# Sums of weight blocks in a Strassen-style gated layer: from VectorE additions to accumulating transfers in place

## The chip, the cores and the metric

The kernel runs on one core of one Trainium2 chip. The metric is the device time in microseconds (us) of one execution; lower is better. The profile is one execution of the same program with the hardware profiler on.

## The reference

A trunk of two layers over 512 tokens of 1024 channels, all in float32. Each layer has a gated feed-forward half step, four groups of attention heads side by side, and a second feed-forward half step, each followed by a normalisation over the channels:

```python
def _swiglu(h, w_gu, w_down):
    gate, up = jnp.split(h @ w_gu, 2, axis=-1)      # w_gu: 1024 x 5632
    return (jax.nn.silu(gate) * up) @ w_down         # w_down: 2816 x 1024

for l in range(DEPTH):                               # DEPTH = 2
    x = _layer_norm(alpha * x + 0.5 * _swiglu(x, ffn_w_gu[l, 0], ffn_w_down[l, 0]), ...)
    mix = _token_mixers(x, w_in[l], ..., w_out[l], l)
    x = _layer_norm(alpha * x + mix, ...)
    x = _layer_norm(alpha * x + 0.5 * _swiglu(x, ffn_w_gu[l, 1], ffn_w_down[l, 1]), ...)
```

The product `h @ w_gu` of the four feed-forward steps is the place of the change.

## The kernel before, in words

**Seven products in place of eight.** A feed-forward step goes through its 2816 hidden columns in 11 *pairs* of 256 columns (44 pairs in all). For one pair the weight is a 2 x 2 arrangement of blocks: rows 0 to 511 and 512 to 1023 of the input channels (first digit 1 and 2) against gate and up columns (second digit 1 and 2). Each block, called b11, b21, b12 and b22, is 128 partitions x 1024 elements in a tile, 512 KB, loaded by a transfer from the SP queue (`Pair.load`, `load`, L93). The token side is split in halves too, and the products are formed by a scheme of Strassen's kind: products 1 to 7 multiply prepared token combinations (`al1` to `al7`, made once per step) with weight combinations w1 to w7. w1 is b11, w2 is b21, w3 is b22, and the other four are sums: w5 = b11 + b12, w6 = b11 + b12 + b22, w7 = b12 + b22, w4 = b21 + w6.

**Two parts of a weight.** TensorE takes each weight combination as a high part (`wh`, a cast on ScalarE, L351) and a low part (`wl`, the difference, on VectorE, L352); `parts4` makes both. They live in rings of four buffers each (`WB`), so a combination can be split as soon as TensorE is through with the product four places earlier. A product is 24 matmuls of 256 columns: for each of two column halves eight with the high part and four with the low part.

**Buffers and queues.** The raw blocks and the sum `t2` share seven slots in turn (`raw_tile`): three of the pool `raw` and four of the tag `pt`. A block's slot is free for the next load when it was split or added for the last time. Each engine carries out its own instructions in program order, the SP and POOL queues too; which order that is, a scheduler decides when the program is built. The pairs follow one another; `prep12` makes w1 and w2, `prep_rest` the other five, `run12` runs products 1 and 2 and `run_rest` the other five.

**Banks.** Product 1 goes to a bank `a` (in the profile `ga`), which ScalarE copies to `s1`; products 6, 7 and 4 are added on top of it, and ScalarE copies it to `u2` between 6 and 7. Product 2 has the bank `gb`. Products 5 and 3 share the bank `gc`, which ScalarE copies to `p5` between the two. A product that adds onto a bank has to wait for the copy taken before it.

The first two pairs of a step are run in an opening of their own: products 1 and 2 of both come first, while the later token combinations are still being made, and the others after that. After the 11 pairs the down product runs (`acc`), then the normalisation, then the next stage. In the attention stages VectorE, ScalarE and POOL share the work; POOL has nothing to do in the 11 pairs.

Of the kernel before, what the change touches and what calls it, by code (L numbers as in the profile page):

```python
# [14 lines left out]
ALU = mybir.AluOpType  # L15
# [7 lines left out]
FF = 2816  # L23
# [49 lines left out]
def tile_encoder(ctx: ExitStack, tc: tile.TileContext, d: dict, out: bass.AP):  # L73
    nc = tc.nc
    ve, se, ge, te = nc.vector, nc.scalar, nc.gpsimd, nc.tensor

    def pool(name, bufs=1, **kw):
        return ctx.enter_context(tc.tile_pool(name=name, bufs=bufs, **kw))

    cst, st, raw, whi, wlo, blk, sm = (pool("cst"), pool("state"), pool("raw"), pool("whi"), pool("wlo"),  # L80
                                       pool("blk"), pool("small"))
    ps = pool("ps", 2, space=PSUM)
    RAW, WB = 3, 4
    BUFS = {"v": 8, "st": 8, "kr": 1, "hl": 10, "nat": 4, "tb": 3, "o": 2, "od": 1, "o2": 2, "p": 6, "oT": 8}
    NPT = 4
    LAG = 3

# [7 lines left out]
    def block(tag, name, dt=F32, width=512):  # L95
        return blk.tile([P, width], dt, tag=tag, name=name, bufs=BUFS[tag])

# [68 lines left out]
    def alk(n, hl, k):  # L166
        for h, l, k0, nk in al[n]:
            if k0 <= k < k0 + nk:
                return (h if hl == "h" else l)[:, k - k0]
# [75 lines left out]
    def cols_of(w):  # L245
        return w.rearrange("(k p) f -> p k f", p=P)

    def mm(o, a, b, start, stop, **kw):
        te.matmul(o, a, b, start=start, stop=stop, **kw)  # L249
        n = 1  # L250
        for w in b.shape[1:]:
            n *= w
        pe[0] += n / 2400.0
# [62 lines left out]

    TAIL = 4
    NB = NC // 2
    HSLOTS = ["oT"] * 8 + ["nat"] * 4 + ["tb"] * 3 + ["hl"] * 6 + ["v"]
    TMP = ["o", "o", "od", "o2", "o2", "kr"]  # L320

    def ffn(l, f, last, to_next):
        wgu = cols_of(d["ffn_w_gu"][l, f])
        wd = d["ffn_w_down"][l, f]
        ring = {"raw": 0, "tmp": 0}
        slots = list(HSLOTS)
        H = []

        def raw_tile(name):

            ring["raw"] += 1
            if ring["raw"] % 7 in (1, 3, 5):
                return raw.tile([P, DM], F32, tag="r", name=name, bufs=RAW)
            return blk.tile([P, DM], F32, tag="pt", name=name, bufs=NPT)

        def tmp(name):
            ring["tmp"] += 1
            return block(TMP[ring["tmp"] % len(TMP)], name)

        def parts4(r, early=None):  # L340

            if early is None:
                h = whi.tile([P, DM], F32R, tag="h", name="wh", bufs=WB)
                lo = wlo.tile([P, DM], F32R, tag="l", name="wl", bufs=WB)
                pieces = [(h, lo, 0, 4)]
            else:
                pieces = [(block(early, "we", F32R), block(early, "we", F32R), k0, 2) for k0 in (0, 2)]
            out_ = []
            for h, lo, k0, nk in pieces:
                q = slice(k0 * 256, (k0 + nk) * 256)  # L350
                se.copy(h, r[:, q])  # L351
                ve.tensor_tensor(lo, r[:, q], h.bitcast(F32), op=ALU.subtract)  # L352
                out_.append(tuple(w.rearrange("p (k c) -> p k c", c=256) for w in (h, lo)) + (k0, nk))
            return out_

        def product(n, o, w, first):

            for c in range(2):
                seq = []
                for h, lo, k0, nk in w:  # L360
                    for k in range(nk):
                        seq += [(h, k, k0 + k, "h"), (h, k, k0 + k, "l")]
                for h, lo, k0, nk in w:
                    for k in range(nk):
                        seq.append((lo, k, k0 + k, "h"))
                for m, (a, k, kk, hl) in enumerate(seq):
                    mm(o[:, c], a[:, k, c * P:(c + 1) * P], alk(n, hl, kk), first and c == 0 and m == 0,
                       c == 1 and m == len(seq) - 1, skip_group_check=True)

        class Pair:  # L370
# [4 lines left out]
                self.j, self.w, self.r = j, {}, {}  # L375

            def load(self, gate=True, up=True):
                j = self.j
                for n, k, u in ((11, 0, 0), (21, 1, 0), (12, 0, 1), (22, 1, 1)):
                    if not (up if u else gate):  # L380
                        continue
                    self.r[n] = raw_tile(f"b{n}")
                    load(self.r[n].rearrange("p (k c) -> p k c", k=4),
                         wgu[:, 4 * k:4 * k + 4, u * FF + j * 256:u * FF + (j + 1) * 256])
                return self

            def prep12(self, early=(None, None)):
                self.w[1] = parts4(self.r[11], early[0])
                self.w[2] = parts4(self.r[21], early[1])
                return self  # L390

            def prep_rest(self):
                r = self.r
                add = lambda o, a, b: ve.tensor_tensor(o, a, b, op=ALU.add)  # L394
                add(r[11], r[11], r[12])
                t2 = raw_tile("t2")
                add(t2, r[11], r[22])
                self.w[6] = parts4(t2)
                self.w[5] = parts4(r[11])
                add(r[12], r[12], r[22])  # L400
                self.w[7] = parts4(r[12])
                self.w[3] = parts4(r[22])
                add(r[21], r[21], t2)
                self.w[4] = parts4(r[21])
                return self

# [13 lines left out]
            def run_rest(self):  # L420
                v3 = lambda t: t.rearrange("p (c t) -> p c t", c=2)
                a = self.a
                product(6, a, self.w[6], False)
                u2 = v3(tmp("u2"))
                se.copy(u2, a)
                c = self.bank("pj", "gc")
                product(5, c, self.w[5], True)
                p5 = v3(tmp("p5"))
                se.copy(p5, c)
                product(7, a, self.w[7], False)  # L430

                ve.tensor_tensor(p5, a, p5, op=ALU.add)
                product(3, c, self.w[3], False)
                se.activation(self.s1, self.s1, AF.Silu, scale=-1.0)

                ve.tensor_tensor(u2, c, u2, op=ALU.add)
                product(4, a, self.w[4], False)
                h0 = v3(block(slots.pop(0), "h0"))
                ve.tensor_tensor(h0, self.s1, u2, op=ALU.mult)
                s2 = v3(tmp("s2"))  # L440
                se.activation(s2, a, AF.Silu, scale=-1.0)
                h1 = v3(block(slots.pop(0), "h1"))
                ve.tensor_tensor(h1, s2, p5, op=ALU.mult)
                H.append((h0, h1))
# [19 lines left out]
        for j in range(2, NB):  # L464
            p = Pair(j).load().prep12().prep_rest()
# [35 lines left out]
        for t in range(NT):  # L501
            for n in range(2):
                for i in range(TAIL):
                    down(t, NC - TAIL + i, ws[i], (n,))
            layer_norm(t, acc[t], 0.5, gb, last and t == NT - 2)
            if last:
                for n in range(2 if t == NT - 1 else 1):
                    sl = slice(n * FD, (n + 1) * FD) if t == NT - 1 else slice(0, DM)
                    load(out[0, t * P:(t + 1) * P, sl], x[t][:, sl])
            else:  # L510
                to_next[1](t)
# [968 lines left out]
    for l in range(DEPTH):  # L1480
        ffn(l, 0, False, (new_xT, to_xT))
        mixer(l)
        ffn(l, 1, l == DEPTH - 1, (new_al, to_al) if l < DEPTH - 1 else None)
# [22 lines left out]
```

## Time and profile before

| | |
|---|---|
| median of 3 runs | 1987.61 us (1985.27 to 1988.29) |
| profiled execution | 1989.4 us, span 1987.6 us from the first to the last instruction |
| mean granted TensorE clock | 0.983 |
| busy: PE / VectorE / ScalarE / POOL | 1906.2 / 1450.0 / 960.0 / 269.5 us |
| additions of L394 | 88 + 44 + 44 on VectorE, 107.4 + 53.6 + 53.6 us |
| transfers, all from the SP queue | 202.49 MB, 33.7% of the 16 DMA engines' span |

The profile names a tile by its name without the number, so b11, b21, b12 and b22 all read `b`, t2 reads `t`, p5 `p`, u2 `u` and s1 `s`. PE is TensorE, PEld its weight loads, DVE VectorE, ACT ScalarE; SPq is the transfer queue of SyncE.

### The profile page before, as it was taken

To read this page: it belongs to the slowest core of one execution; us is meant where nothing else is said; L and a number is where in the kernel's file an instruction comes from. 1 tells how busy PE (TensorE), PEld (TensorE's weight loads), DVE (VectorE), ACT (ScalarE), POOL (GpSimd) and SP (SyncE) were. 2 spreads that over 40 slices of the span, in tenths; PEclk is the share of its full clock that TensorE was granted. 3 is DMA by queue.
4 is the path that set the end of the run, shared out by engine and by line. 5 is a ranking of instruction groups with operands and counts; after the bars stand their busy time and mean duration, and the time that the engine had idled before them with its cause. 6 is when DMAs were issued, how large, how long until landed. Compare 5 with 4: busy or idle time off the path is not lost.

```text
span 1987.6 us, 31884 instructions
## 1 busy us (share of the span) xinstructions
PE 1906.2 (96%) x12396; PEld 1735.7 (87%) x12396; DVE 1450.0 (73%) x2229; ACT 960.0 (48%) x1593; POOL 269.5 (14%) x411
## 2 busy tenths in 40 slices
PE   7999999999999899999999999999999979999998
PEld 6999988788887899988889999887887869999886
DVE  7887742858999978763598787337689998878535
ACT  5544532248774554443155545322587745444421
POOL 0000000335741000000000000004366300000001
PEclk9999999999999899999999999999999989999999
DMA  5323233343442333332223323331533424232321
GB/s 196 120 88 115 97 101 105 86 112 89 112 112 86 96 110 103 107 127 96 85 77 106 121 92 99 110 120 47 141 93 92 118 74 128 92 112 84 106 97 62
DMA packets 156487, 204.53 MB, mean 103 GB/s; under 512 B 14064, under 2 KB 122608, under 8 KB 156336
## 3 DMA queue, kind: packets, MB, share of 16 engines
q1 hardware_dynamic: 156336, 202.49, 33.7%
q8 instruction: 98, 1.61, 0.3%
q14 instruction: 53, 0.43, 0.1%
HBM read 177.42 MB, written 2.10 MB: 90 GB/s over the span
## 4 chain that ended last, share of the span: by engine, by line
PE 85%; DVE 8%; POOL 2%; ACT 2%; issue 2%; DMA 1%; SPq 0%; DVEq 0%; POOLq 0%; ACTq 0%
PE ga L249 25%; PE acc L249 23%; PE gc L249 13%; PE gb L249 6%; PE nat L249 5%; PE op L249 3%; PE sc L249 3%; PE pjt L249 2%; PE pv L249 2%; PE ptb L109 2%; DVE p L591 1%; PE xtp L109 1%; DVE al L178 1%; POOL wl L222 0%; DVE x L314 0%
## 5 line engine op out<-in xcount | busy, mean ns | idle before, releaser
L249 PE MATMUL ga<-al,wh 128*128 128x256 f32 x2752 | 392.5, 285 | 12.4 <-ACT wh L351 11.7
L351 ACT CAST wh<-b 128x1024 fp32r<-128x1024 f32 x256 | 267.7, 1049 | 280.2 <-issue 164.7
L352 DVE TENSOR_TENSOR wl<-b,wh 128x1024 fp32r<-128x1024 f32 x256 | 311.2, 1219 | 120.9 <-ACT wh L351 120.9
L249 PEld LDWEIGHTS ga<-al,wh 128*128 128x128 f32 x2752 | 360.2, 194 | 13.0 <-ACT wh L351 12.1
L222 DVE TENSOR_TENSOR wl<-wr,wh 128x1024 fp32r<-128x1024 f32 (+1 forms) x92 | 112.2, 1220 | 232.1 <-ACT wh L221 232.1
L249 PE MATMUL acc<-wh,hh 128*128 128x512 f32 x704 | 272.9, 390 | 6.7 <-ACT hh L480 6.7
L249 PE MATMUL acc<-wh,hl 128*128 128x512 f32 x704 | 276.6, 393 | 1.1 <-DVE hl L481 1.1
L249 PE MATMUL acc<-wl,hh 128*128 128x512 f32 x704 | 276.5, 393 | 0.2 <-DVE wl L222 0.2
L221 ACT CAST wh<-wr 128x1024 fp32r<-128x1024 f32 (+2 forms) x98 | 101.5, 1040 | 269.1 <-PE acc L249 226.0
L249 PE MATMUL ga<-al,wl 128*128 128x256 f32 x1376 | 224.3, 286 | 0.0
L303 POOL TENSOR_SCALAR rs<-mv 128x1 f32<-128x1 f32 x24 | 9.9, 412 | 1498.8 <-DVE mv L301 1498.7
L249 PE MATMUL gc<-al,wh 128*128 128x256 f32 x1408 | 201.1, 285 | 4.6 <-ACT al L177 4.3
L249 PEld LDWEIGHTS ga<-al,wl 128*128 128x128 f32 x1376 | 192.2, 194 | 0.6 <-DVE wl L352 0.3
L249 PEld LDWEIGHTS gc<-al,wh 128*128 128x128 f32 x1408 | 184.3, 194 | 5.2 <-ACT al L177 4.5
L249 PEld LDWEIGHTS acc<-wh,hh 128*128 128x128 f32 x704 | 132.1, 188 | 34.5 <-ACT hh L480 7.5
L249 PEld LDWEIGHTS acc<-wh,hl 128*128 128x128 f32 x704 | 133.3, 189 | 30.3 <-DVE hl L481 2.8
L249 PEld LDWEIGHTS acc<-wl,hh 128*128 128x128 f32 x704 | 133.1, 189 | 28.4 <-DVE wl L222 0.6
L249 PE MATMUL gc<-al,wl 128*128 128x256 f32 x704 | 113.6, 284 | 0.0
L394 DVE TENSOR_TENSOR b<-b,b 128x1024 f32<-128x1024 f32 x88 | 107.4, 1220 | 5.5 <-DMA b<-in_ffn_w_gu_dram 4.2
L249 PEld LDWEIGHTS gc<-al,wl 128*128 128x128 f32 x704 | 97.6, 193 | 0.0
L351 ACT CAST wh<-t 128x1024 fp32r<-128x1024 f32 x44 | 46.2, 1049 | 105.6 <-DVE t L394 105.6
L249 PE MATMUL gb<-al,wh 128*128 128x256 f32 x640 | 90.8, 285 | 0.0
(280 smaller groups left out, 3414.6 us busy)
## 6 DMA issues: line engine op xcount, KB each, us to landing
b<-in_ffn_w_gu_dram SPq DMA_DIRECT2D x176, 512.0 KB, 3.6
wr<-in_ffn_w_down_dram SPq DMA_DIRECT2D x88, 512.0 KB, 3.2
wr<-in_w_in_dram SPq DMA_DIRECT2D x30, 512.0 KB, 3.7
k<-ph SPq DMA_DIRECT2D x64, 128.0 KB, 2.4
wr<-in_w_out_dram SPq DMA_DIRECT2D x16, 512.0 KB, 3.6
qs<-ph SPq DMA_DIRECT2D x32, 128.0 KB, 2.4
ln_g<-in_ln_g_dram SPq DMA_DIRECT2D x12, 256.0 KB, 4.1
ln_b<-in_ln_b_dram SPq DMA_DIRECT2D x12, 256.0 KB, 4.7
```

The costliest lines, as they stand in the source:

```text
L109: te.transpose(o, a, ident)
L178: ve.tensor_tensor(l[:, :, cs], v, h[:, :, cs].bitcast(F32), op=ALU.subtract)
L221: se.copy(h[:, w], r[:, w])
L222: (lo or ve).tensor_tensor(l[:, q], r[:, q], h[:, q].bitcast(F32), op=ALU.subtract)
L249: te.matmul(o, a, b, start=start, stop=stop, **kw)
L303: ge.tensor_scalar(rs[:, 0:1], mv[:, 1:2], 1.0, EPS * INV_A * INV_A, op0=ALU.mult, op1=ALU.add)
L351: se.copy(h, r[:, q])
L352: ve.tensor_tensor(lo, r[:, q], h.bitcast(F32), op=ALU.subtract)
L394: add = lambda o, a, b: ve.tensor_tensor(o, a, b, op=ALU.add)
L591: ve.tensor_tensor_reduce(p, sb, nd, -h.slope, h.sink[0] if h.sink else 3.0e38, ALU.add, ALU.min, m)
```

## The change

The four sums are no longer formed by VectorE. Each is an accumulating transfer that POOL issues: it adds its source onto what is in the destination tile. Three of the four read a block of the weights from device memory again, the fourth reads a tile on the chip. The tile `t2` is gone: b11 becomes w5 in place and then w6 in place. `prep_rest` is written in another order, and `run_rest` has product 5 ahead of product 6. One buffer of the tag `hl` is given up, and one more of the tag `v` takes its place in `HSLOTS`; `dynamic_dma_scratch_size`, the room for the descriptors of POOL's transfers, goes from 256 to 2048.

```diff
-    BUFS = {"v": 8, "st": 8, "kr": 1, "hl": 10, ...}
+    BUFS = {"v": 8, "st": 8, "kr": 1, "hl": 9, ...}
...
-    HSLOTS = ["oT"] * 8 + ["nat"] * 4 + ["tb"] * 3 + ["hl"] * 6 + ["v"]
+    HSLOTS = ["oT"] * 8 + ["nat"] * 4 + ["tb"] * 3 + ["hl"] * 5 + ["v"] * 2
...
+            def src(self, u, k):
+                return wgu[:, 4 * k:4 * k + 4, u * FF + self.j * 256:u * FF + (self.j + 1) * 256]
...
+            def add(self, n, src):
+                ge.dma_start(self.r[n].rearrange("p (k c) -> p k c", k=4), src, accum_op=ALU.add)
+
             def prep_rest(self):
-                r = self.r
-                add = lambda o, a, b: ve.tensor_tensor(o, a, b, op=ALU.add)
-                add(r[11], r[11], r[12])
-                t2 = raw_tile("t2")
-                add(t2, r[11], r[22])
-                self.w[6] = parts4(t2)
+                r, b12, b22 = self.r, self.src(1, 0), self.src(1, 1)
+                self.add(12, b22)
+                self.add(11, b12)
                 self.w[5] = parts4(r[11])
-                add(r[12], r[12], r[22])
+                self.add(11, b22)
+                self.w[6] = parts4(r[11])
+                self.add(21, r[11].rearrange("p (k c) -> p k c", k=4))
                 self.w[7] = parts4(r[12])
                 self.w[3] = parts4(r[22])
-                add(r[21], r[21], t2)
                 self.w[4] = parts4(r[21])
...
             def run_rest(self):
-                product(6, a, self.w[6], False)
-                u2 = v3(tmp("u2"))
-                se.copy(u2, a)
                 c = self.bank("pj", "gc")
                 product(5, c, self.w[5], True)
                 p5 = v3(tmp("p5"))
                 se.copy(p5, c)
+                product(6, a, self.w[6], False)
+                u2 = v3(tmp("u2"))
+                se.copy(u2, a)
                 product(7, a, self.w[7], False)
```

ScalarE before, from the split of w7 of one pair (blocks b11_1145, b21_1147, b12_1149, b22_1151) to that of w1 of the next (b11_1373). Behind a tile's name is its number; in brackets are the counters that the instruction waits for (DMAHW a transfer of the SP queue, DMASW one of POOL's):

```order
L351 CAST wh_1173<-b12_1149 128x1024 [waits DMAHW0_49,PE_49,Activation_49]
L414 COPY s1_1211<-ga_1186 128x512 [waits PE_49]
L351 CAST wh_1177<-b22_1151 128x1024 [waits DMAHW1_49,PE_49,Activation_49]
L434 ACTIVATE s1_1211<-s1_1211 128x512 [waits DVE_49]
L351 CAST wh_1182<-b21_1147 128x1024 [waits PE_49,Activation_49]
L425 COPY u2_1263<-ga_1186 128x512 [waits PE_49]
L351 CAST wh_1381<-b11_1373 128x1024 [waits DMAHW2_49,PE_49,Activation_49]
L429 COPY p5_1290<-gc_1265 128x512 [waits PE_49]
```

ScalarE after, the same stretch of the same pair (now b11_1141, b21_1143, b12_1145, b22_1147; the next pair's b11_1368 and b21_1370), and on to the split of that pair's w5:

```order
L351 CAST wh_1169<-b12_1145 128x1024 [waits DMASW6_49,PE_49,Activation_49]
L417 COPY s1_1206<-ga_1181 128x512 [waits PE_49]
L351 CAST wh_1173<-b22_1147 128x1024 [waits DMAHW2_49,PE_49,Activation_49]
L437 ACTIVATE s1_1206<-s1_1206 128x512 [waits DVE_49]
L351 CAST wh_1177<-b21_1143 128x1024 [waits DMASW4_49,PE_49,Activation_49]
L429 COPY p5_1259<-gc_1234 128x512 [waits PE_49]
L351 CAST wh_1376<-b11_1368 128x1024 [waits DMAHW3_49,PE_49,Activation_49]
L432 COPY u2_1285<-ga_1181 128x512 [waits PE_49]
L351 CAST wh_1380<-b21_1370 128x1024 [waits DMAHW1_49,PE_49,Activation_49]
L351 CAST wh_1386<-b11_1368 128x1024 [waits DMASW5_49,DVE_49,PE_49]
```

The cast of w4 (wh_1177) now waits for a transfer of POOL's, and both copies of the pair's banks and the cast of the next pair's w1 stand behind it; p5 and u2 have changed places.

POOL after, from the first sum on b11 of that pair on (before, POOL had no row between the start of the program and the first normalisation):

```order
L395 DMA b11_1141<-in_ffn_w_gu_dram 128x4x256 [waits DMAHW2_49,DMAHW6_49,DMASW1_49,DVE_49]
L395 DMA b12_1372<-in_ffn_w_gu_dram 128x4x256 [waits DMAHW4_49,DMASW0_49]
L395 DMA b11_1141<-in_ffn_w_gu_dram 128x4x256 [waits DMASW1_49,DVE_49]
L395 DMA b21_1143<-b11_1141 128x1024 [waits DMAHW7_49,DMASW3_49]
L395 DMA b11_1368<-in_ffn_w_gu_dram 128x4x256 [waits DMAHW5_49,DMAHW3_49,DVE_49]
L395 DMA b12_1599<-in_ffn_w_gu_dram 128x4x256 [waits DMAHW0_49,DMASW6_49,DMASW4_49]
L395 DMA b11_1368<-in_ffn_w_gu_dram 128x4x256 [waits DMASW5_49,DVE_49]
L395 DMA b21_1370<-b11_1368 128x1024 [waits DMAHW1_49,DMASW7_49]
```

The first sum on a b11 waits for VectorE (the split of w1), the second for the first one's landing and the split of w5, and the sum on b21 for the second one's landing; the sum on the next pair's b12 stands between the first two.

TensorE after, at the products of the same pair: the end of product 6 (bank ga_1181), product 3 (gc_1234) and the first matmul of product 7 (ga_1181). The first row of product 3 needs the copy p5, the first of product 7 the copy u2:

```order
L249 MATMUL ga_1181<-al6_92,wl_1165 128x256 x4
L249 MATMUL gc_1234<-al3_102,wh_1173 128x256 [waits Activation_49]
L249 MATMUL gc_1234<-al3_103,wh_1173 128x256
L249 MATMUL gc_1234<-al3_102,wh_1173 128x256
L249 MATMUL gc_1234<-al3_103,wh_1173 128x256
L249 MATMUL gc_1234<-al3_104,wh_1173 128x256
L249 MATMUL gc_1234<-al3_105,wh_1173 128x256
L249 MATMUL gc_1234<-al3_104,wh_1173 128x256
L249 MATMUL gc_1234<-al3_105,wh_1173 128x256
L249 MATMUL gc_1234<-al3_102,wl_1174 128x256 [waits DVE_49]
L249 MATMUL gc_1234<-al3_102,wl_1174 128x256
L249 MATMUL ga_1181<-al7_93,wh_1169 128x256 [waits Activation_49]
```

Before, the products of a pair stood whole in the order 1, 2, 6, 5, 7, 3, 4; now it is 1, 2, 5, 6, ten matmuls of 3, 7, the other fourteen of 3, and 4.

VectorE before, at the end of the opening of the second step (pair 0 is b11_7005, b21_7007, b12_7009, b22_7011):

```order
L418 TENSOR_TENSOR s1_7119<-gb_7121,s1_7119 128x512 [waits PE_49]
L394 TENSOR_TENSOR b11_7005<-b11_7005,b12_7009 128x1024 [waits DMAHW4_49]
L668 TENSOR_SCALAR nsink_13858<-sink_13857 128x4
L685 TENSOR_SCALAR gd_13869<-gd_13869 128x1
L394 TENSOR_TENSOR t2_7156<-b11_7005,b22_7011 128x1024 [waits DMAHW3_49,DVE_49]
L394 TENSOR_TENSOR b12_7009<-b12_7009,b22_7011 128x1024
L394 TENSOR_TENSOR b21_7007<-b21_7007,t2_7156 128x1024 [waits DVE_49]
L352 TENSOR_TENSOR wl_7159<-t2_7156,wh_7158 128x1024 [waits Activation_49]
```

VectorE after, at the same place (pair 0 is b11_6994, b21_6996, b12_6998, b22_7000):

```order
L421 TENSOR_TENSOR s1_7108<-gb_7110,s1_7108 128x512 [waits PE_49]
L352 TENSOR_TENSOR wl_7147<-b11_6994,wh_7146 128x1024 [waits DMASW5_49]
L671 TENSOR_SCALAR nsink_13825<-sink_13824 128x4
L688 TENSOR_SCALAR gd_13836<-gd_13836 128x1
L352 TENSOR_TENSOR wl_7152<-b11_6994,wh_7151 128x1024 [waits DMASW0_49,Activation_49]
L352 TENSOR_TENSOR wl_7157<-b12_6998,wh_7156 128x1024 [waits DMASW4_49,Activation_49]
```

The four additions are gone, and the low part of w5 stands first where they began; the next one, w6, waits for a transfer that can only start after that.

More of the change, by code (lines that the diff above doesn't have):

```diff
@@ L83, in tile_encoder @@
     RAW, WB = 3, 4
-    BUFS = {"v": 8, "st": 8, "kr": 1, "hl": 10, "nat": 4, "tb": 3, "o": 2, "od": 1, "o2": 2, "p": 6, "oT": 8}
+    BUFS = {"v": 8, "st": 8, "kr": 1, "hl": 9, "nat": 4, "tb": 3, "o": 2, "od": 1, "o2": 2, "p": 6, "oT": 8}
     NPT = 4
@@ L377, in load @@
             def load(self, gate=True, up=True):
-                j = self.j
                 for n, k, u in ((11, 0, 0), (21, 1, 0), (12, 0, 1), (22, 1, 1)):
@@ L382, in load @@
                     self.r[n] = raw_tile(f"b{n}")
-                    load(self.r[n].rearrange("p (k c) -> p k c", k=4),
-                         wgu[:, 4 * k:4 * k + 4, u * FF + j * 256:u * FF + (j + 1) * 256])
-                return self
+                    load(self.r[n].rearrange("p (k c) -> p k c", k=4), self.src(u, k))
+                return self
+            def src(self, u, k):
+                return wgu[:, 4 * k:4 * k + 4, u * FF + self.j * 256:u * FF + (self.j + 1) * 256]
             def prep12(self, early=(None, None)):
@@ L1492 @@
     from concourse.bass_utils import run_bass_kernel_spmd as _run
-    nc = _bacc.Bacc("TRN2", target_bir_lowering=False, num_devices=1, dynamic_dma_scratch_size=256)
+    nc = _bacc.Bacc("TRN2", target_bir_lowering=False, num_devices=1, dynamic_dma_scratch_size=2048)
     arrays, args = {}, {}
```

## Prediction, made before the changed kernel was run

> **What bounds the kernel now.** I read the page's head, then a table by stages, then the chain of work that ended last. First the span, the busy time of each engine, and two stretches of 180 us, one inside the eleven pairs of the first feed-forward step and one inside those of the second:
>
> ```profile
> span 1987.6 us, 31884 instructions
> ...
> PE 1906.2 (96%) x12396; PEld 1735.7 (87%) x12396; DVE 1450.0 (73%) x2229; ACT 960.0 (48%) x1593; POOL 269.5 (14%) x411
> ...
> 60.00:240.00 180.00, 180.00 (x1503) 180.00 (x1502) 142.57 (x146) 91.38 (x113) 0.00 (x0) 1.00 0.32 97
> ...
> 680.00:860.00 180.00, 180.00 (x1503) 180.00 (x1502) 144.97 (x149) 91.22 (x112) 0.00 (x0) 1.00 0.35 108
> ```
>
> The columns of the last two lines are busy us of PE, its weight loads, DVE, ACT and POOL, then granted clock, DMA share and GB/s. In the pairs PE has no gap at all and VectorE is busy 143 of 180 us. So VectorE is not what sets the pace there, and what is taken off it brings nothing by itself. The chain shows the pace, from product 2 of one pair to product 2 of the next:
>
> ```profile
> 107.41 2.88 PE gb L249 x24
> 110.29 2.88 PE ga L249 x24
> 113.17 2.88 PE gc L249 x24
> ...
> 127.57 2.88 PE gb L249 x24
> ```
>
> A product takes 2.88 us and a pair 127.57 - 107.41 = 20.16 us. The open question is whether the sums still come in time at that pace. Outside the steady pairs PE's waits for the work of this change are few; the list of waits (total, times, longest) has
>
> ```profile
> PE xtp L109 <- DVE x L314: 21.4, 8, 6.5
> PE ga L249 <- ACT wh L351: 11.7, 2, 6.0
> ```
>
> The second line is two openings of a step, where the split of w6 comes late behind VectorE's additions.
>
> **What is removed.** Groups by line, with count, busy us and mean ns:
>
> ```profile
> L352 DVE TENSOR_TENSOR wl<-b,wh 128x1024 fp32r<-128x1024 f32 x256 | 311.2, 1219 | 120.9 <-ACT wh L351 120.9
> ...
> L351 ACT CAST wh<-b 128x1024 fp32r<-128x1024 f32 x256 | 267.7, 1049 | 280.2 <-issue 164.7 <-PE ga L249 92.6 <-ACT hh L480 16.4
> ...
> L394 DVE TENSOR_TENSOR b<-b,b 128x1024 f32<-128x1024 f32 x88 | 107.4, 1220 | 5.5 <-DMA b<-in_ffn_w_gu_dram 4.2
> ...
> L394 DVE TENSOR_TENSOR t<-b,b 128x1024 f32<-128x1024 f32 x44 | 53.6, 1219 | 0.1
> L394 DVE TENSOR_TENSOR b<-b,t 128x1024 f32<-128x1024 f32 x44 | 53.6, 1219 | 0.0
> ```
>
> The three L394 groups go: 107.4 + 53.6 + 53.6 = 214.6 us of VectorE, all under a PE without gaps except in the openings. Worth 0 in the steady pairs.
>
> **What is added: three transfers in a row per pair.** By the order of instructions, the second sum on b11 needs the first landed and w5 split, the sum on b21 needs the second landed, and ScalarE has the cast of w4, which needs the sum on b21, ahead of the copy p5, the next pair's cast of w1 and the copy u2. The next pair's first sum on b11 needs w1 split. That closes a loop from pair to pair: cast w4 1.05, copy p5 0.58, cast w1 1.05, difference w1 1.22, transfer, cast w5 1.05, difference w5 1.22, transfer, transfer. The engine part is 6.17 us; 1.05 and 1.22 are from the groups above, 0.58 from
>
> ```profile
> L429 ACT COPY p<-gc x44: 582/582/587, 41.2 to 1847.6; 128x512 f32<-128x512 f32 x44
> ```
>
> With S the sum of the three transfers from issue to landing, the loop takes S + 6.17. It is hidden while that is at most 20.16, so up to S = 14.0, 4.7 us for each. The fourth sum, on b12, is outside the loop: its load is ordered before it is needed and w7 is the fifth product.
>
> No accumulating transfer and none from POOL is in the trace. The nearest rows (KB each, median us from issue to landing), and POOL's own operations:
>
> ```profile
> b<-in_ffn_w_gu_dram SPq DMA_DIRECT2D x176, 512.0 KB, 3.6
> wr<-in_ffn_w_down_dram SPq DMA_DIRECT2D x88, 512.0 KB, 3.2
> ...
> nd_d<-in_nd_d_dram SPq DMA_DIRECT2D x1, 448.0 KB, 9.4
> ...
> 628.13 0.56 POOL L304 TENSOR_TENSOR rs<-rs,mhalf 128x1 f32<-128x1 f32 x1
> ```
>
> From below: a sum costs what the plain load costs, 3.6 from the weights, and 3.2 for the sum on b21, whose rows are 4 KB like those of the second line: S = 10.4. From above: the slowest load of about this size, 9.4 each: S = 28.2. I take a value nearer to the lower end, since the plain loads have the same size, rows and destination. On top of them comes a second pass over 512 KB, because the old content must be read to be added to: the line of 680 to 860 us gives 108 GB/s at a share of 0.35, so 309 GB/s at full share, and 512 KB take 1.7 us. For POOL's issue I add one small operation of its own, 0.56. That is 5.86, 5.86 and 5.46, together 17.2. Of the transfers outside the loop (four loads and the sum on b12) some fall on it: the slot of the next b11 is free when w4 is split, just as the first sum starts, so I add one load's 1.7. S = 18.9, the loop 25.1 us, 4.9 more than a pair takes now.
>
> The Trainium skill ("Collectives: The Full Stack", the section on the bandwidth ceiling) says that an add in the DMA engines costs no cycles but two source reads, which halves the rate; that agrees with taking a second pass, and no run here shows it yet. Its page "DMA: Bandwidth & Descriptors", in the section on the anatomy of a POOL-issued transfer, fits such a transfer as 2.0 us plus bytes at 436 GB/s; an estimate from both is 4.4 us each, 13.2 in all, and the loop would stay just hidden, which is the first rival below. The rows give the dearer answer, and I stay with them.
>
> **How often.** Pairs 1 to 10 of a step are tied by nine loops, 36 in the four steps: 36 x 4.9 = 176 us. In pair 1, w5 can be split only after product 6 of pair 0 (its buffer); from there w5 2.27, two transfers 11.3, w4 1.05 and p5 0.58 make 15.2, against five products, 14.4: 0.8, four times, 3 us.
>
> **The openings.** The end of the second step's opening, VectorE and then TensorE:
>
> ```profile
> 657.16 0.69 DVE L418 TENSOR_TENSOR s<-gb,s 128x512 f32<-128x512 f32 x1
> 657.76 1.22 DVE L394 TENSOR_TENSOR b<-b,b 128x1024 f32<-128x1024 f32 x1
> ...
> 659.03 1.22 DVE L394 TENSOR_TENSOR t<-b,b 128x1024 f32<-128x1024 f32 x1
> 660.16 1.22 DVE L394 TENSOR_TENSOR b<-b,b 128x1024 f32<-128x1024 f32 x1
> 661.29 1.22 DVE L394 TENSOR_TENSOR b<-b,t 128x1024 f32<-128x1024 f32 x1
> ...
> 661.37 2.08 PE L249 MATMUL ga<-al,wh 128*128 128x256 f32 x8 [6.04 <-ACT wh L351]
> ```
>
> Here the additions do hold PE up, 6.04 us. After the change the difference of w5 stands where they began and ends at 658.98; product 5 can run meanwhile. But the second sum is issued only then: it lands 5.86 later at 664.84, and w6 is cast at 665.9, so product 6 ends at 668.8. Before, products 6 and 5 were through at 661.37 + 5.76 = 667.1. Product 7 then waits for the copy u2 behind the cast of w4: 664.84 + 5.46 + 1.05 + 0.58 = 671.9, against 668.8 + 1.2 for the ten matmuls of product 3. Loss 1.7 + 1.9 = 3.6, for three openings 11 us. The first step's additions come early, between its loads; 0 there.
>
> **Side effects at nothing.** POOL has no other work in the pairs; its part of the normalisation stands behind sums of the next step whose inputs are loaded in the stage before, so it hides under that stage's matmuls, and if that cover went each of four normalisations would be late by a transfer. SP issues the same loads in about the same order. A PE that pauses is granted less clock:
>
> ```profile
> 650.00:660.00 10.00, 5.33 (x37) 4.96 (x35) 10.00 (x17) 4.77 (x9) 0.00 (x0) 0.84 0.00 1
> 660.00:670.00 10.00, 8.63 (x55) 8.51 (x56) 8.60 (x9) 6.01 (x7) 0.00 (x0) 0.72 0.48 138
> ```
>
> 0.84 and 0.72 around that 6 us gap. The loop has no matmul in it, so slower matmuls eat slack first: 0.
>
> **Sum.** 176 + 3 + 11 = 190 us on the profiled execution's 1989.4, so 2179.4. The median of the runs shown is 1.8 lower than that execution: 2178.
>
> **Rivals.** *Hidden.* The three transfers take at most 14.0 us. For it: the plain loads land in 3.2 to 3.6. Against it: each has to gain no more than 1.2 us over them, with a second pass, software issue and other traffic. Then the steady pairs keep 20.16 and the openings decide; at 3.6 per transfer w6 is cast at 663.6 and product 6 ends at 666.5, 0.6 earlier than now. About 1988. 13%. *Faster.* The place is the same opening: if product 5 fills PE's wait wholly and w6 follows without a stall, the 11.7 us of PE waiting for L351 go, and the time is 1976. It needs the second sum landed before product 5 ends (about 661 us), so about 2 us after issue, less than any 512 KB row shows; only an earlier split of w5 than the order gives could do it. 7%. *The transfers themselves are the limit.* Per pair there are four loads and four sums; at two passes a sum that is 12 x 1.7 = 20.4 us of all 16 engines, already a pair's time. If the adding path moves at half the rate, or POOL's descriptors take as long as the transfer, the landings come to the upper row, 9.4: the loop is 34.4 us, 14.2 x 36 = 513, with the openings about 2520. For it: the share is 0.35 now, and the loads queue behind the sums. Against it: no row in the pairs is that slow. 18%. That the sums stay on VectorE is excluded: its order of instructions has no addition of blocks left.
>
> **Chances and range.** The forecast, the loop late by a few us, has 62%; with S from 15 to 24 it spans 36 x 1.0 to 36 x 10.0 on top of 1988 and the openings, 2030 to 2360. The range reaches down to the hidden case and up into the third rival: 1984 to 2470, leaving out the faster case and the slower half of the third. A measurement here can tell about 0.2% (4 us): slower by more 0.80, within 0.13, faster 0.07.
>
> **What would show it.** Right: POOL's transfers land 5 to 6 us after issue; PE waits once per pair ahead of product 3 for the copy p5 (L429), ScalarE ahead of it for the sum on b21 at the cast of w4; the pair takes about 25 us, VectorE's busy time falls by 215 us, DMA share in the pairs nears 0.8. Wrong: the pair stays at 20.16 us (landings under 4.7), or landings of 8 us and more with the DMA engines full. A loop through a buffer or a bank that I have left out would lengthen the pair at the same landings.

## The result, and the profile after

The changed kernel takes 2411.7 us (median), against 1986.96 us before: 1.213 times as long, interval 1.209 to 1.217, 425 us more. One of its four executions took 5532 us and is not in the ratio; the other three took 2405.8 to 2416.9 (median 2406.5). The forecast was 2178 us, 190 us more; the direction and the range held, the size did not. The profiled execution took 2416.9 us, with a span of 2414.9 us.

The page of the changed kernel: span, busy time of the engines, and the transfers that POOL and SP issue (KB each, median us from issue to landing):

```profile
span 2414.9 us, 32159 instructions
...
PE 2022.7 (84%) x12396; PEld 1831.3 (76%) x12396; DVE 1258.0 (52%) x2053; ACT 950.7 (39%) x1593; POOL 479.5 (20%) x587
...
b<-in_ffn_w_gu_dram SPq DMA_DIRECT2D x176, 512.0 KB, 5.6
b<-in_ffn_w_gu_dram POOLq DMA_DIRECT2D x132, 512.0 KB, 6.1
...
b<-b POOLq DMA_DIRECT2D x44, 512.0 KB, 4.4
```

VectorE is 192 us less busy, and PE, which had no gap in the pairs, now waits; its busy time is 117 us longer for the same 12396 matmuls, at a lower granted clock (0.84 below, 1.00 before). The same stretch of the first step as was shown of before (busy us of PE, its weight loads, DVE, ACT and POOL, granted clock, DMA share, GB/s):

```profile
60.00:240.00 180.00, 137.18 (x1000) 134.60 (x1000) 70.21 (x78) 57.82 (x73) 28.16 (x24) 0.84 0.67 142
```

No engine is full there, nor are the DMA engines at 0.67. Before, TensorE ran 1503 matmuls in these 180 us, now 1000. The chain is therefore made of waits. The timeline of POOL in one pair (start, duration, in brackets the idle time before and what ended it):

```profile
116.93 1.30 POOL L395 DMA_DIRECT2D b<-in_ffn_w_gu_dram  x1 [8.34 <-DVE wl L352]
124.65 1.30 POOL L395 DMA_DIRECT2D b<-in_ffn_w_gu_dram  x1 [6.42 <-DMA b<-in_ffn_w_gu_dram]
131.11 1.29 POOL L395 DMA_DIRECT2D b<-in_ffn_w_gu_dram  x1 [5.16 <-issue]
137.92 0.89 POOL L395 DMA_DIRECT2D b<-b  x1 [5.52 <-issue]
147.42 1.30 POOL L395 DMA_DIRECT2D b<-in_ffn_w_gu_dram  x1 [8.61 <-DVE wl L352]
```

By the order of instructions these are the first sum on b11, the sum on the *next* pair's b12, the second sum on b11, the sum on b21, and the next pair's first sum. By the trace they land at 124.34, 130.79, 137.35 and 142.36. The second sum on b11 waits in the program only for the first one and for VectorE, whose difference of w5 ends at 126.75, yet it is issued at 131.11, 0.32 us after b12's sum has landed. b12's sum itself is issued 0.31 us after the first one has landed, though its own load was there at 121.75. What ended the second sum's wait reads "issue": nothing that the program waits for. (b21's row reads the same, but there the program does wait for the second sum, which landed 0.57 us earlier.) So b12's 6.46 us lie between the two sums on b11; w5 is split during them, and 4.4 us are lost. The loop is 30.5 us instead of the 25.1 of the forecast.

TensorE, ScalarE and DVE in the same pair, from product 2 (bank gb) of this pair to that of the next:

```profile
126.19 1.12 PE L249 MATMUL gb<-al,wh 128*128 128x256 f32 x8
...
137.43 1.99 ACT L351 CAST wh<-b 128x1024 fp32r<-128x1024 f32 x2 [11.45 <-DMA b<-in_ffn_w_gu_dram]
139.33 0.58 ACT L417 COPY s<-ga 128x512 f32<-128x512 f32 x1
139.96 2.08 PE L249 MATMUL ga<-al,wh 128*128 128x256 f32 x8 [7.85 <-ACT s L417]
...
142.46 1.05 ACT L351 CAST wh<-b 128x1024 fp32r<-128x1024 f32 x1 [0.32 <-DMA b<-b]
...
142.69 1.91 PE L249 MATMUL ga<-al,wh 128*128 128x256 f32 x8
143.41 0.58 ACT L429 COPY p<-gc 128x512 f32<-128x512 f32 x1
...
144.68 1.05 ACT L351 CAST wh<-b 128x1024 fp32r<-128x1024 f32 x1 [0.68 <-ACT p L429]
...
156.68 1.12 PE L249 MATMUL gb<-al,wh 128*128 128x256 f32 x8
```

Product 2 comes 30.5 us later than the one before. PE stands still 7.85 us ahead of product 6 (bank ga), behind ScalarE's copy s1, which stands behind the casts of w6 and w7; w6 had to wait 11.45 us for the second sum. Over the whole execution PE's list of waits (total, times, longest) has as its first line of this kind

```profile
PE ga L249 <- ACT s L417: 178.8, 27, 8.8
```

The account, from the start of product 2 in each pair, over the four steps and in us:

| stretch | before | after | difference | forecast |
|---|---|---|---|---|
| product 2 of pair 2 to that of pair 10, 32 intervals | 645 (20.16 each) | 987 (30.86 each) | 342 | 157 |
| from there to the end of the down product | 569 | 588 | 19 | 20 |
| up to product 2 of pair 2, from the start or from the last step's down product | 764 | 830 | 66 | 14 |

(The forecast's 36 loops of 4.9 us are 32 in the first row and four in the second.)

### The profile page after: what moved, and what is told of

Its sections match the earlier page's. It is cut to its first block, busy times and chain, and to the rows that moved or that the text cites. A ratio compares the mean times of both kernels' runs of the same rounds, so it can differ in the third digit from the quotient of the medians.

```text
span 2414.9 us, 32159 instructions
## 1 busy us (share of the span) xinstructions
PE 2022.7 (84%) x12396; PEld 1831.3 (76%) x12396; DVE 1258.0 (52%) x2053; ACT 950.7 (39%) x1593; POOL 479.5 (20%) x587
## 3 DMA queue, kind: packets, MB, share of 16 engines
q0 software_dynamic: 76032, 92.29, 24.6%
## 5 line engine op out<-in xcount | busy, mean ns | idle before, releaser
L352 DVE TENSOR_TENSOR wl<-b,wh 128x1024 fp32r<-128x1024 f32 x300 | 361.3, 1222 | 615.1 <-ACT wh L351 615.1
L249 PE MATMUL ga<-al,wh 128*128 128x256 f32 x2752 | 452.7, 314 | 234.0 <-ACT s L417 178.8
L351 ACT CAST wh<-b 128x1024 fp32r<-128x1024 f32 x300 | 307.5, 1045 | 766.6 <-DMA b<-in_ffn_w_gu_dram 591.6
L249 PEld LDWEIGHTS ga<-al,wh 128*128 128x128 f32 x2752 | 410.5, 220 | 248.4 <-ACT s L417 184.3
L395 POOL DMA_DIRECT2D b<-in_ffn_w_gu_dram x132 | 172.0, 1303 | 1019.2 <-DVE wl L352 331.6
L249 PE MATMUL gc<-al,wh 128*128 128x256 f32 x1408 | 217.1, 300 | 69.1 <-ACT wh L351 32.1
L249 PEld LDWEIGHTS gc<-al,wh 128*128 128x128 f32 x1408 | 197.6, 207 | 74.0 <-ACT wh L351 33.9
L249 PE MATMUL ga<-al,wl 128*128 128x256 f32 x1376 | 245.5, 306 | 0.0
L249 PEld LDWEIGHTS ga<-al,wl 128*128 128x128 f32 x1376 | 215.1, 216 | 0.7 <-DVE wl L352 0.6
L613 POOL TENSOR_SCALAR p<-p,l 128x512 f32<-128x512 f32 (+2 forms) x96 | 66.0, 691 | 140.0 <-DVE l L612 97.1
```

Source lines behind the costliest of these rows:

```text
L395: ge.dma_start(self.r[n].rearrange("p (k c) -> p k c", k=4), src, accum_op=ALU.add)
L613: ge.tensor_scalar(b.p[0], b.p[0], l[:, 3:4], 1.0, op0=ALU.mult, op1=ALU.mult)
```

## Experiments

All numbers are against the kernel before, 1984 to 1986 us in these comparisons. "A pair" is the mean of the 32 intervals of the table's first row: 20.16 us before, 30.86 in the changed kernel. Diffs are against the changed kernel unless said otherwise.

**Room for descriptors.** The theory: a transfer of POOL's is not issued before the room for its descriptors is free, so b12's sum is a link of the loop. Twice the room, paid for with one buffer of the tag `hl`; and a control that gives up the buffer but keeps the room at 2048:

```diff
-    BUFS = {... "hl": 9, ...};  HSLOTS = [...] + ["hl"] * 5 + ["v"] * 2
+    BUFS = {... "hl": 8, ...};  HSLOTS = [...] + ["hl"] * 4 + ["v"] * 3
-    nc = _bacc.Bacc(..., dynamic_dma_scratch_size=2048)
+    nc = _bacc.Bacc(..., dynamic_dma_scratch_size=4096)     # the control keeps 2048
```

> All four sums stay transfers; the room for the descriptors of POOL's transfers goes from 2048 to 4096, paid for with one more buffer of the tag hl. In the changed kernel each transfer of POOL's is issued 0.3 us after the one ahead of it landed, the b12 sum too, which needs no other sum: pairs 2 to 10 take 30.85 us each (32 intervals between products 2, 987.3 us). Theory room: a 512 KB sum fills more than half of the descriptor room, so the next one cannot be issued before the first is through, and b12's 6.1 to 6.5 us count in the loop. With twice the room b12 is issued right behind the first sum on b11, the loop is 16.6 + 6.2 = 22.8 us and what the two cost each other, say 23 to 26 us a pair; 32 x 6 = 190 us less, about 2160 to 2250 us. Rival queue: POOL's accumulating transfers go one after the other whatever the room; the pair keeps its 30.8 us and the time 2412 us within 10. Rival traffic: the DMA engines are full (share 0.67); then two sums at once only land later, and the time stays at 2390 or more with landings of 9 us and more.

> The same buffers as in the run with 4096, the room left at 2048. It tells the price of the buffer alone: every theory expects the changed kernel's 2412 us within 10.

Measured: 2262.9 us with 4096, ratio 1.139 (1.136 to 1.142), a pair 27.1 us; the control 2406.3 us, ratio 1.213 (1.210 to 1.215), a pair 30.7. The buffer costs nothing, the room brings 143 us, a little less than expected (2160 to 2250 us). POOL with 4096, same place of the program:

```profile
122.02 1.30 POOL L395 DMA_DIRECT2D b<-in_ffn_w_gu_dram  x1 [7.85 <-DVE wl L352]
126.12 1.30 POOL L395 DMA_DIRECT2D b<-in_ffn_w_gu_dram  x1 [2.81 <-DMA b<-in_ffn_w_gu_dram]
132.13 1.29 POOL L395 DMA_DIRECT2D b<-in_ffn_w_gu_dram  x1 [4.71 <-DVE wl L352]
138.42 0.89 POOL L395 DMA_DIRECT2D b<-b  x1 [4.99 <-DMA b<-in_ffn_w_gu_dram]
147.68 1.30 POOL L395 DMA_DIRECT2D b<-in_ffn_w_gu_dram  x1 [8.37 <-DVE wl L352]
```

b12's sum is issued at 126.12, while the first sum is under way (it lands at 129.31), and the second sum waits for the difference of w5 as the program has it. This pair takes 25.7 us, near the forecast's 25.1. The mean is higher because some pairs take longer, three of 30 to 32 us in the first step. There the scheduler put b12's sum ahead of the first sum on b11, and the first sum waits behind it for b12's load.

**b12's sum out of the loop, in three ways.** On VectorE; behind the first sum on b11, with 4096; behind the sum on b21, with 2048:

```diff
-                self.add(12, b22)
+                ve.tensor_tensor(r[12], r[12], r[22], op=ALU.add)
```
```diff
-                self.add(12, b22)
-                self.add(11, b12)
+                first = self.add(11, b12)
+                with tc.issue_after(behind[0]): self.add(12, b22)   # from pair 1 on
...
+                behind[:] = [first]      # the pair before; in the third way its sum on b21
```

> Only the sum on b12 goes back to VectorE (44 additions of 1.22 us); the three sums of the chain stay transfers, the room stays 2048. Theory room and rival queue alike: b12's transfer leaves POOL's order, where it stood between the two sums on b11, and with it 6.1 + 0.4 us of every loop; 6.1 + 6.1 + 4.4 + 6.2 = 22.8 us a pair, 32 x 8 = 256 us less, about 2130 to 2180 us. Rival 'b12 is outside the loop', as the prediction had it: the pair keeps 30.8 us, and 2412 us within 15. Rival traffic: a sum less is 3 x 512 KB of about 16 x 512 KB less to move, a fifth; the pair falls to about 26 us, 2250 us.

> The run with 4096 of room, and POOL's order changed at its three exceptions in each step: there the sum on the next pair's b12 stood ahead of the first sum on b11 and made the pair 30 to 32 us (199.75 and 200.74, then the second sum only at 211.81); now it is always issued behind that first sum. In the run with 4096 the other pairs take 24.2 to 25.6 us. Theory loop (the prediction's, with b12 really outside): every pair takes about 25.4 us, 18 to 20 us less per step than with 4096 alone, 2263 - 60 = about 2190 to 2215 us. The theory that other buffers or the loads are a second loop: the exceptions stay at 28 us or more, and the time above 2240.

> Room 2048 as in the changed kernel; the sum on the next pair's b12 is issued only behind the sum on b21, not between the two sums on b11. With one transfer at a time, it then lies beside the engine part of the loop (w4, p5, w1: 4 to 5 us) and holds the next first sum up by only 6.1 + 0.3 - 4.5 = about 2 us. Theory room: 25.4 + 2 = 27 to 28 us a pair, about 2260 to 2310 us. If the place in POOL's order did not matter: 2412.

Measured: 2249.9 us, ratio 1.134 (1.132 to 1.136), a pair 26.75; 2218.9 us, 1.117 (1.115 to 1.119), a pair 25.75; and 2269.5 us in one execution, a pair 26.7. The first misses its 2130 to 2180 us, the second lies 4 us above its 2190 to 2215, the third is within 2260 to 2310. Wherever the second sum on b11 need not wait for the landing of b12's, 140 to 190 us go; in the second way b12's sum still stands between the two sums on b11, but finds room. "b12 is outside the loop" is refuted by all three, and "one after the other whatever the room" by the run with 4096. The third shows that not the number of transfers counts but how many packets they take; POOL there, at 2048:

```profile
146.34 0.90 POOL L396 DMA_DIRECT2D b<-b  x1 [5.04 <-DMA b<-in_ffn_w_gu_dram]
147.00 1.56 POOL L396 DMA_DIRECT2D b<-in_ffn_w_gu_dram  x1
```

b12's sum is issued right behind that on b21, which is still moving. The page of the run with b11 alone (below) has 46464 packets for its 88 sums from the weights, 528 each; the 76032 of the changed kernel leave 6336 for the 44 sums on b21, 144 each. So 528 + 144 packets fit in 2048 and two transfers of 528 do not; in 4096 they do. (How the room's unit converts to packets, no run shows.) The next first sum, at 156.52, again comes 0.32 us behind the landing of that b12's sum. The Trainium skill ("DMA: Bandwidth & Descriptors", the section on terms) says that the descriptors of such a transfer are written to rings in the SBUF. No run here shows where they lie; what the runs show is that POOL's queue stands still until there is room.

The run with b12 on VectorE should have come to 22.8 us a pair and came to 26.75. Its VectorE shows why:

```profile
123.36 1.23 DVE L399 TENSOR_TENSOR b<-b,b 128x1024 f32<-128x1024 f32 x1 [3.13 <-DMA b<-in_ffn_w_gu_dram]
124.50 1.22 DVE L352 TENSOR_TENSOR wl<-b,wh 128x1024 fp32r<-128x1024 f32 x1
126.14 1.32 POOL L395 DMA_DIRECT2D b<-in_ffn_w_gu_dram  x1 [11.89 <-DVE wl L352]
```

The addition on the next b12 stands ahead of the difference of w1 and waits for the load of b22, whose slot is b11's of this pair and comes free only with the sum on b21. The first sum waits behind both: another loop, through a load.

**The other links of the loop.** Only the two sums on b11 as transfers; only that on b21 on VectorE:

```diff
-                self.add(12, b22)
+                ve.tensor_tensor(r[12], r[12], r[22], op=ALU.add)       # not in the second run
-                self.add(21, r[11].rearrange("p (k c) -> p k c", k=4))
+                ve.tensor_tensor(r[21], r[21], r[11], op=ALU.add)
```

> The two sums on b11 stay transfers, those on b12 and b21 are VectorE's; room 2048. By the prediction's loop: two transfers 6.1 + 6.1, an addition of 1.22 in place of the third, and the engine part 6.2: 19.6 us, so just hidden under 20.16; with the 1.5 us of small waits that the run with 4096 shows beyond the engine part, 21.1. Theory loop: pairs of 20.2 to 22 us, 1995 to 2060 us. If instead every sum as a transfer costs the pairs its own share, two of four leave about half of 425 us: 2150 to 2200. What VectorE's order alone can do (an addition placed ahead of a difference and waiting for a load, as in the run with b12 on VectorE) would show as pairs of 24 us and more, with VectorE waiting for a load ahead of the addition on b12.

> Only the sum on b21 goes back to VectorE; the sums on b12 and b11 stay transfers, room 2048. By the prediction's loop the third transfer of the chain goes (4.4 us, and 0.6 until it is issued) and an addition of 1.22 comes: 3.8 us less per loop, 36 x 3.8 = 137 us less, about 2275 us. Rival, from the run with b11's two alone: ScalarE has five rows between the split of w6 and that of w4 (w6, w7, s1, w3 and the activation of s1, 1.05 + 1.05 + 0.58 + 1.05 + 0.63 = 4.4 us and its waits), which run while the sum on b21 is moved; the third transfer lies beside them and costs nothing, so the time stays at 2390 to 2420 us.

Measured: 2226.0 us, ratio 1.121 (1.120 to 1.123), a pair 26.5, a clear miss of the 1995 to 2060 expected; and 2383.0 us, ratio 1.202 (1.199 to 1.204), a pair 30.5, where the prediction's loop gave 2275 and its rival 2390 to 2420, nearly met. ScalarE, VectorE and PE with b11's two sums alone, after the second has landed at 137.35:

```profile
137.38 1.23 DVE L404 TENSOR_TENSOR b<-b,b 128x1024 f32<-128x1024 f32 x1 [3.98 <-DMA b<-in_ffn_w_gu_dram]
137.43 1.99 ACT L351 CAST wh<-b 128x1024 fp32r<-128x1024 f32 x2 [4.87 <-DMA b<-in_ffn_w_gu_dram]
139.80 1.05 ACT L351 CAST wh<-b 128x1024 fp32r<-128x1024 f32 x1
142.04 1.03 ACT L351 CAST wh<-b 128x1024 fp32r<-128x1024 f32 x1
142.69 1.16 PE L249 MATMUL ga<-al,wh 128*128 128x256 f32 x8
142.98 0.58 ACT L429 COPY p<-gc 128x512 f32<-128x512 f32 x1
143.34 1.23 DVE L400 TENSOR_TENSOR b<-b,b 128x1024 f32<-128x1024 f32 x1 [0.74 <-DMA b<-in_ffn_w_gu_dram]
143.93 1.05 ACT L351 CAST wh<-b 128x1024 fp32r<-128x1024 f32 x1 [0.37 <-ACT p L429]
147.25 1.29 POOL L395 DMA_DIRECT2D b<-in_ffn_w_gu_dram  x1 [14.73 <-DVE wl L352]
```

The sum on b21 is there at 138.6, but w4 is cast only at 142.04: ScalarE first casts w6 and w7, copies s1, casts w3 and activates s1. With the transfer it was cast at 142.46, 5.11 us after the second sum had landed; now 4.69. The third transfer lies beside ScalarE's own rows and is worth about 0.4 us a pair, not the 3.8 that the prediction's loop gives it.

The cast of the next pair's w1 waits for something else again. Its high part goes into the buffer that held that of w6, four places earlier in the ring, so product 6 must be through with it. Here the last matmuls of product 6 that read it end at 143.85 (142.69 + 1.16), and the cast starts at 143.93, though the copy p5 ahead of it had ended at 143.56. In the changed kernel they end at 144.60 and the cast starts at 144.68, with the copy done at 143.99; the trace puts that wait down to the copy. Of the 31 places in the changed kernel where this cast stands right behind that copy, 23 show the same. So product 6, which follows w6, w7 and s1 on ScalarE, is a link of the loop, and it runs at a low clock: granted 0.59 between 138 and 146 us in the changed kernel, 0.79 in this run.

From the second landing to the next first sum it is 9.90 us here (137.35 to 147.25), against 10.07 with all four sums as transfers. The difference of w1 is another 0.6 us late here: VectorE's addition on the next b12 (143.34) stands ahead of it and waits for that load. The rest of the miss is the first sum, which lands 7.8 us after its issue in this pair.

**Traffic or order?** POOL's transfers as plain copies (the sums are left out), and all four sums with 4096 but the next pair's w1 and w2 split ahead of w4:

```diff
-                ge.dma_start(..., src, accum_op=ALU.add)
+                ge.dma_start(..., src)
```
```diff
-            p = Pair(j).load().prep12().prep_rest()
-            p.run12()
+            q = Pair(j).load().prep12()
+            p.prep4()                       # the split of w4, taken out of prep_rest
             p.run_rest()
+            p = q
+            p.prep_rest(False)
+            p.run12()
```

> The changed kernel with POOL's four transfers per pair as plain copies: they overwrite what is in the destination instead of adding to it, so the sums are left out; all else, order and waits, is the same. It prices the second read. If the second pass over 512 KB costs 1.7 us, as the prediction added, the landings fall from 6.1 to 4.4 us (and 4.4 to 2.7 for the sum on b21), S with b12 by 6.8 us a pair: 32 x 6.8 = 218 us less, about 2200 us. If POOL's writing of descriptors and the way to the engines is the whole price, the landings stay at 5.7 us or more and the time above 2350 us.

> All four sums stay transfers, room 4096, the same traffic; only the order of the code is another: the split of the next pair's w1 and w2 is written ahead of that of w4, so that on ScalarE the cast of w1 no longer stands behind the cast of w4 and POOL can issue the next first sum sooner. Theory loop: the loop is now first sum 6.1, w5 2.85, second sum 6.1, then w6, w7, s1, w3, the activation and w1 on ScalarE 5.4 and the difference 1.2, 21.7 to 23 us a pair: with 36 loops and some 45 us of openings about 2085 to 2140 us. Rival traffic (the DMA engines or POOL cannot move four sums and four loads in less than about 25 us): 25 us or more a pair, 2200 us or more.

Measured: 2043.7 us, ratio 1.030 (1.026 to 1.034), a pair 21.65 (several of 20.4); and 2143.1 us, ratio 1.079 (1.078 to 1.080), a pair 23.9. The landings of the plain copies:

```profile
b<-in_ffn_w_gu_dram POOLq DMA_DIRECT2D x132, 512.0 KB, 4.2
...
b<-b POOLq DMA_DIRECT2D x44, 512.0 KB, 2.9
```

Against 6.1 and 4.4, adding costs 1.9 and 1.5 us of a landing; the prediction had 1.7. (In the first of the two the number of packets changes too.) That agrees with the two source reads that the Trainium skill ("Collectives: The Full Stack", the section on the bandwidth ceiling) gives for an add in a transfer, but the landing as a whole does not double. The plain time is lower than the 2200 expected, since a plain copy takes 144 packets (25344 for 176) and b12's fits beside the first one at 2048: POOL issues it at 129.74, and the one before lands at 131.45.

In the run with w1 split early the four sums and four loads stay, and the pair falls by 3.2 us against the run with 4096. It is also 1.8 under the 25.75 of the run with b12 behind the first sum. So order, not traffic, set those. Two things in the order differ: in five pairs of each step the scheduler also put b12's sum right behind the second sum on b11. The pair missed its 21.7 to 23 by the first sum on b11, which now lands 6.6 to 8.2 us after issue, and by the way from the second landing to the next first sum, 7.4 us instead of 6.6. Here the transfers do get crowded (columns as above):

```profile
100.00:240.00 140.00, 128.20 (x1024) 124.86 (x1022) 68.50 (x73) 58.13 (x73) 29.21 (x26) 0.99 0.88 184
```

**What else the change holds.** b12 alone as a transfer; no transfer at all, only the new order and buffers (the four `add` calls as VectorE additions in place); and the kernel before with two of its four additions as transfers:

```diff
-                add(r[12], r[12], r[22])                                # of the kernel before
+                ge.dma_start(r[12]..., <b22 in device memory>, accum_op=ALU.add)
-                add(r[21], r[21], t2)
+                ge.dma_start(r[21]..., t2..., accum_op=ALU.add)
```

> Only the sum on b12 is a transfer; the other three are VectorE's additions, in the order and with the buffers of the changed kernel. No loop from pair to pair holds a transfer: POOL issues b12's sum when both its load and VectorE's first sum on b11 (which reads b12) are through, and w7 is the third of the five products. The pairs should be at 20.16 us again, VectorE 54 us less busy than before, and the time 1975 to 2000 us. If a transfer of POOL's costs the pairs anything by itself (POOL's writing of descriptors, or traffic), it shows as pairs above 20.2 us.

> No transfer from POOL at all: the four sums are VectorE's, in place as in the changed kernel (b11 becomes w5 and then w6, no t2), product 5 ahead of 6, and the changed kernel's buffers. It tells what the order and the buffers cost without the transfers. Where b12 alone was a transfer the time was 2001 us, pairs of 20.4. If that was the transfer's, this run is back at 1985 within 4; if the order's, it is at 1995 to 2005 too.

> The kernel before, with its t2, its order of products and its first two additions on VectorE; only the sums on b12 and b21 are transfers (the latter from t2), with room 2048. Nothing of the loop holds a transfer: b12 and b21 are the fifth and the last split of a pair. VectorE loses 88 of 176 additions, 107 us. Theory: the pairs stay at 20.16 to 20.4 us; in the openings the difference of w6 comes up to 2.4 us earlier, so 1975 to 1990 us. If every transfer of POOL's costs a pair 0.2 us by itself, 1995 or more.

Measured: 2001.2 us, ratio 1.008 (1.007 to 1.010), a pair 20.41; 1998.1 us, 1.006 (1.005 to 1.008), a pair 20.41; 1991.8 us, 1.003 (1.002 to 1.004), a pair 20.16. The new order and buffers cost 12 us by themselves, 0.25 a pair; what b12's transfer adds, some 3 to 5 us, is hardly clear of the intervals. TensorE shows the 0.25 with no transfer in the program:

```profile
743.92 1.12 PE L249 MATMUL gc<-al,wh 128*128 128x256 f32 x8
744.88 0.40 PE L249 MATMUL gc<-al,wl 128*128 128x256 f32 x2
745.27 1.22 PE L249 MATMUL ga<-al,wh 128*128 128x256 f32 x8
```

Product 7 starts behind ten matmuls of product 3 and still has to wait for the copy u2: 745.27 - 744.88 is 0.39 for two matmuls that take 0.24 elsewhere, and the eight behind them take 1.22 in place of 1.12. The last run has no loop through a transfer and the old order: 88 of VectorE's 176 additions are gone, the pairs are exactly as before, and nothing is won, since VectorE was not what they waited for. The gain expected in the openings (1975 to 1990 us) did not come either. No version here is faster than the kernel before.

## Why the prediction came out too low

**What bounds, and what is removed: right.** The pairs ran at TensorE's pace, and taking additions off VectorE brought nothing; the last run shows it at unchanged pairs.

**The loop of b11 and b21: near in size, wrong in two links.** With b12 out of it the forecast was 25.1 us, and the run with b12 behind the first sum has 25.75. The terms in the pair of the run with 4096: first sum 7.29 (5.86 + 1.7 of collision forecast), w5 2.82 (2.27), second sum 5.99 (5.86), b21 0.30 + 4.43 (5.46), then 4.83 (3.90). One wrong link is that everything behind the second sum hangs on b21's transfer: ScalarE's rows between w6 and w4 take as long. The other is "the loop has no matmul in it": the cast of the next w1 waits for product 6, slower at its low clock, and in the changed kernel it starts 0.69 us later than the copy p5 would let it. That the size comes out near is in part luck, then: the way over product 6 is about as long as the one over b21's transfer. So "hidden up to S = 14.0" does not hold either: two sums on b11 alone gave 26.5 us a pair.

**"The fourth sum, on b12, is outside the loop": this is the step that failed.** It looked at whether b12's sum would be in time, not at what it does to POOL's queue, where it stands between the two sums on b11. At 2048 the second b11 sum cannot be issued before it has landed. With it out of the way (2218.9) the change costs 234 us, with it 422 in the run with the same buffers (2406.3): 188 of the 234 us by which the forecast was short. Of these 188 the room gives 143 with b12 where the scheduler put it; two or three times a step it stood ahead of the first sum even so, which is the other 44 (2262.9 to 2218.9).

**The openings: too small, 66 against 14.** Of the 66, 28 are the first step's opening, where POOL's queue was taken as free; it shrinks to 9.5 in the run with b12 behind the first sum. Of the other 38, about 20 lie ahead of the second and the fourth step, at POOL's part of the normalisation, put at nothing under "side effects"; 18 are the three openings, where 11 was forecast. POOL ahead of the second step in the changed kernel:

```profile
741.62 1.29 POOL L395 DMA_DIRECT2D b<-in_ffn_w_gu_dram  x1 [7.57 <-DVE x L307]
748.11 1.28 POOL L395 DMA_DIRECT2D b<-in_ffn_w_gu_dram  x1 [5.19 <-issue]
749.46 0.19 POOL L303 TENSOR_SCALAR rs<-mv 128x1 f32<-128x1 f32 x1
```

The normalisation's small operation stands behind a sum that waits for room, and VectorE's last step of the normalisation (L314) waits 9.3 us for it, ahead of the fourth step as well. The prediction named this price ("late by a transfer") and took the cover to hold. The 12 us of the new order, which the prediction gave no term, are no part of the error: a wait of 0.25 us for u2 counts only where the pairs run at TensorE's pace.

**What would show it.** Landings of 6.1 and 4.4 (5 to 6 said), 192 us less on VectorE (215 said) and a DMA share of 0.67 (0.8 said) are near what was said. PE's wait came not ahead of product 3 for p5 but ahead of product 6 for s1. The pair was longer than forecast at slightly shorter transfers, S = 16.6 against 17.2 without collision, and the prediction had named that sign of an overlooked loop; it thought of a buffer or a bank, and most of it was a queue.

**The rivals.** "The transfers themselves are the limit" gave 2520 (its 14.2 x 36 is 511, not 513) and so came nearer in time than the forecast, but not by its mechanism: landings are 6.1, not 9.4, the DMA share is 0.67, and the same four sums in another order took 2143. "Hidden" and "faster" are refuted by every run that has the sums on b11 as accumulating transfers.

## What to carry to other kernels

An operation moved to another queue must be placed in that queue, not only among its data: ask which transfers stand ahead of and behind it, and whether two of them fit in the room for descriptors at once, counting packets (528 for a sum from 1 KB rows in the weights, 144 for one from a tile). A sum in place by transfers turned an addition of 1.22 us into a link of 6 us whose operands come from other engines, and it tied the next pair to this one; look for that loop before pricing its links, for the other engines whose rows lie beside a link, and for the rings of buffers that bring one more engine into it. Where the engine that is relieved is not waited for, as VectorE in the pairs here, the best that can come of it is no change.

## What the runs showed of the hardware

POOL's issue of a 512 KB transfer takes 1.30 us for a sum from the weights, 0.89 for one from a tile and 0.75 for a plain copy from the weights. A transfer that waits for room for its descriptors goes out 0.3 us after an earlier one has landed, and POOL's later instructions wait with it, small operations of the normalisation among them (9.3 us); the trace calls that wait "issue" in some rows. A sum from the weights goes in 528 packets, one from a tile and a plain copy in 144, and the loads of SP land after 5.6 us instead of 3.6, of which the new order alone gives 4.5 (the run without a transfer of POOL's).
